# A hybrid decoder layer: the input of chunks 1 to 3 turned by VectorE, the norm's factor applied after the projections

## The chip, the cores and the metric

The kernel runs on one core of a Trainium2 chip. The metric is the device time of one execution in microseconds (us). TensorE (PE, with its weight loads as PEld), VectorE (DVE), ScalarE (ACT), GpSimd (POOL) and SyncE (SP, which issues most of the transfers) each work through a queue of instructions in its written order.

## The reference

One layer on x (1 x 2048 x 1024, float32), cut to what matters:

```python
h = rms_norm(x, attn_norm_g)                  # x * rsqrt(mean(x*x)) * g
z = h @ w_in                                  # q 512, k 128, v 128, gate_b 512, gate_c 512, xc 512
q, k = rms_norm(q, q_norm_g), rms_norm(k, k_norm_g)
y_attn = swa_sink_attention(q, k, v, sinks)   # 8 heads of 64, 2 kv heads, window 128
y_conv = gate_b * short_conv(gate_c * xc, conv_w)      # 3 taps, causal
y = concat(rms_norm(y_attn, attn_out_g), rms_norm(y_conv, conv_out_g))
x = x + y @ w_out
hm = rms_norm(x, mlp_norm_g)
x = x + square(relu(hm @ w_up)) @ w_down      # w_up 1024x4096
```

A matrix product is made in three terms: both operands are split into a high part (rounded to the matmul's type) and a low part (what the rounding left), and `mm3` adds high x high, high x low and low x high in PSUM.

## The kernel before

The sequence is cut into four chunks of CH = 512 tokens, each of NT = 4 tiles of P = 128 rows. Features lie in KD = 8 groups of 128. For each chunk (0 to 3) the "mixers" phase makes the projection, the attention of four blocks, the gated convolution and the out projection. After it come the MLP's up product (line L1401) and down product (L1508), which take the last 70% of the time and which the change does not touch.

The projections need h of a chunk turned, with features on the partitions: two parts (high and low, `h_h`) of 128 x 8 x 512. They have one buffer each, and the convolution of the present chunk reads them to its last matmul (`pb_c`), so h of the next chunk is written after that. `prepare` makes it for chunks 1 to 3. For each of the four row tiles it fetches 128 x 1024 of x in one transfer (`xt_a`, two buffers), has ScalarE take the sum of squares (L273) and GpSimd the reciprocal root, multiplies by the norm's factor and the gain row on VectorE (L280), turns the tile by eight 128x128 transposes on TensorE in two groups of four (`pt_a`, L292, one PSUM bank), copies each group to the high part on ScalarE (L296) and subtracts on VectorE for the low part (L297). Chunk 0 is made apart, at the start: there the transposes are of x itself, the gain is applied in the copy, and the norm's factor (`rs0`) multiplies the projections' outputs; its square lies as a row over the tokens on all partitions (`rs0_row`).

`besides` runs the convolution, `prepare`, the second half of the out projection and the next chunk's projection as a stream of small steps. `mixers` interleaves it with the attention's steps (`fill`). The attention of one block: queries and keys turned (`ptq_b`, `ptk_b`), scores (`psc_b`) copied by ScalarE, masked by VectorE (L646), exponentials by ScalarE (L652), normalised by VectorE (L660), turned (`ptp_b`) and split into `pp_b` (ScalarE L677, VectorE L678) with GpSimd's masks on it (L684), values (`po_b`, L723) and their split. The convolution: gate C (`pc_c`, copied by ScalarE at L773 in chunks 1 to 3, multiplied by `rs0_row` on VectorE in chunk 0), `px_c`, the three taps on VectorE (L790, L792), gate B (`pb_c`), the split `yt_c` (L807, L808), the sum of squares `ssc` (L812, L813).

Weights are read in chunk 0 as raw parts (`raw_wc`, `raw_wx`, `raw_wb`, `raw_wo`), split by ScalarE (L243, L246) and VectorE (L247) into `w_...`, and stored; later chunks read the stored parts (lines L226 to L230). The out projection is `pout`, made in two halves; each result is added to x on VectorE with the branch's norm factor (`rc` for the convolution's, L862).

The order of each engine's queue is set when the kernel is built, by a planner that has its own costs. Steps within `with ahead(i)` have a priority from a table by stage, and the program's order breaks ties. No order is decided while the kernel runs: an engine waits at the instruction that stands next in its queue, and a transfer behind a waiting transfer on SP waits with it.

Of the kernel before, what the change touches and what calls it, by code (L numbers as in the profile page):

```python
# [7 lines left out]
F32 = mybir.dt.float32  # L8
# [4 lines left out]
ALU = mybir.AluOpType  # L13
# [55 lines left out]

CHP = CH + 32  # L70
STEPS = 3
REST = 7
LATER = 250

# [27 lines left out]
def hymba_layer(  # L102
# [44 lines left out]
        [[dram.tile([P, 2, BW], F32, name=f"fop{tb}_{i}_{g}") for g in range(NCG // 2)] for i in range(len(ORDER))]  # L147
        for tb in range(NTB)
    ]
    wds_dram = [[dram.tile([P, 2, BW], F32, name=f"wds{g}_{i}") for i in range(2)] for g in range(NCG // 2)]  # L150

    def bank(tag, name):
# [126 lines left out]
    def scaled(xt, rs, gb):  # L279
        nc.vector.scalar_tensor_tensor(xt, xt, rs, gb, op0=ALU.mult, op1=ALU.mult)  # L280

    def norm(xt, gb, name):

        scaled(xt, norm_stats(xt, name), gb)

    def transposed(xt, dst, t, name, tag="tr"):

        for kk in range(0, KD, 4):
            with ahead(9):
                pt = bank(tag, f"pt_{name}_{kk}")  # L290
                for j in range(4):
                    nc.tensor.transpose(pt[:, j * P : (j + 1) * P], xt[:, (kk + j) * P : (kk + j + 1) * P], ident)  # L292
                p3 = pt.rearrange("p (k t) -> p k t", k=4)
                dh = dst[0][:, kk : kk + 4, t * P : (t + 1) * P]
                dl = dst[1][:, kk : kk + 4, t * P : (t + 1) * P]
                nc.scalar.copy(dh, p3)  # L296
                nc.vector.tensor_tensor(dl, p3, dh.bitcast(F32), op=ALU.subtract)  # L297
            yield

    def raised(xt, dst, name, tag="tr"):  # L300

        for k in range(2):
# [12 lines left out]
    def x_sums(tb, t, b11, b21, b12, b22, t1):  # L315
# [17 lines left out]
    def parts(pool_, tag, name):  # L333
        return [pool_.tile([P, KD, CH], F32R, tag=f"{tag}{s}", name=f"{tag}{s}_{name}", bufs=1) for s in range(2)]

    def prepare(src, r0, gb, dst, name):

        xs = []

        def fetch(t):  # L340
            xt = row("xt", f"xt_{name}_{t}", 2)
            nc.sync.dma_start(xt, src[r0 + t * P : r0 + (t + 1) * P, :])
            with ahead(8):
                norm(xt, gb, f"{name}_{t}")
                xs.append(xt)
# [168 lines left out]
    with tc.tile_pool(name="mix_small", bufs=1) as mix_small, tc.tile_pool(name="mix", bufs=1) as mix:  # L514
# [10 lines left out]
        def project_qkv(c, h, z):  # L525
# [36 lines left out]
            w4 = [w.rearrange("p (k c) -> p k c", k=KD) for w in weights(None, c, "qkv2")]  # L562

            for pc, t in ((0, 0), (0, 1), (1, 0), (0, 2), (0, 3), (1, 1), (1, 2), (1, 3)):
                n = 256 if pc else AW
                ps = bank("mm", f"pz{c}_{pc}_{t}")[:, :n]
                hk = lambda s, k, t=t: h[s][:, k, t * P : (t + 1) * P]
                wk = (lambda s, k: w4[s][:, k, :]) if pc else (lambda s, k: both[k // (KD // 2)][s][:, k % (KD // 2), :])
                for k in range(KD):
                    mm3(ps, lambda s, k=k: hk(s, k), lambda s, k=k: wk(s, k), k == 0, k == KD - 1)  # L570
                    if (k % 2 or not pc) and k < KD - 1:
                        yield
                nc.scalar.copy(z[t][:, pc * AW : pc * AW + n], ps)
                if pc and not t:
                    qk_norm(c * NT, z[0])
                yield
# [169 lines left out]
            nc.vector.tensor_copy(ms, pa[:, :1])  # L746
            rsqrt(dst, ms)

        def conv_pair(c, h, j, yt, ssc):

            nm = f"c{c}_{j}"

# [15 lines left out]
            for i in range(2):  # L768
                ps = bank("mm", f"pc_{nm}_{i}")
                yield from group(hl, ps, i)  # L770
                g = pool.tile([P, CHP], F32, tag="s2", name=f"u_{nm}_{i}", bufs=4)
                if c:
                    nc.scalar.copy(g[:, 2 : CH + 2], ps)  # L773
                else:
                    nc.vector.tensor_tensor(g[:, 2 : CH + 2], ps, rs0_row, op=ALU.mult)
                gc.append(g)
                yield
            hl = weights(cols256(wi, O_X + j * 256), c, f"wx{j}")
# [127 lines left out]
                    x_put(0, t, 2, b[1])  # L906
                yield

        def besides(c, before, h, yt, rc, x1, h_next, z_next):
# [11 lines left out]
            out = out_projection(c, 1, yt, rc, x1)  # L921
            if c + 1 < NCHUNK:
                h_next += parts(pool, "h", f"h{c + 1}")
                steps = prepare(xf, (c + 1) * CH, g_row[0], h_next, f"a{c + 1}")
            else:
                steps = prepare_mlp(gain_row(mlp_norm_g, "g_mlp"))
            for i, _ in enumerate(steps):
                yield
                for j in range(STEPS):
                    next(out, None)  # L930
                    yield
                    if (i, j) == PC:
# [5 lines left out]
                        ms = mix_small.tile([P, NT], F32, tag="msc", name=f"ms_c{c}", bufs=1)  # L938

                        with tc.high_priority(offset=SOON):  # L940
                            if c:
                                nc.vector.tensor_copy(ms, pc[:, :NT])
                                rsqrt(rc, ms)
                            else:
                                nc.vector.tensor_tensor(ms, pc[:, :NT], rs0_2, op=ALU.mult)
                                rsqrt(rc, ms)
                                nc.gpsimd.tensor_tensor(rc, rc, rs0, op=ALU.mult)
            yield from out
            if c + 1 < NCHUNK:
                yield from project_qkv(c + 1, h_next, z_next)  # L950
            else:
                begin_mlp()

        def mixers(c, before, h, z):


            last = c + 1 == NCHUNK
            n_fill = FILL[c]
            stage[0] = c
            at, yt, x1, h_next, z_next = [], [], [], [], []  # L960
            ra = small.tile([P, NT], F32, tag="ra", name=f"ra{c}", bufs=2)
            rc = small.tile([P, NT], F32, tag="rc", name=f"rc{c}", bufs=2)
            steps = besides(c, before, h, yt, rc, x1, h_next, z_next)
            left = out_projection(c, 0, at, ra, x1)

            spare = (NT - 1) * NCT if last else 0
# [43 lines left out]
                        attn_rstd(b, sqa, ra[:, NT - 1 : NT])  # L1010
                    yield

            return rest(), h_next, z_next

        z = []
        for _ in project_qkv(0, h, z):
# [39 lines left out]
        g_row = [gain_row(attn_norm_g, "g_attn")]  # L1056
        left = iter(())
        for c in range(NCHUNK):
            left, h, z = mixers(c, left, h, z)
        for _ in left:  # L1060
            pass

# [485 lines left out]
```

## Time and profile before

| what | us |
| --- | --- |
| median of 3 runs | 1944.46 |
| the runs, lowest to highest | 1941.45 to 1945.74 |
| span of the profiled execution, first to last instruction | 1937.4 |
| median less that span | 7.1 |
| TensorE busy | 1921.2 |
| VectorE busy | 1192.2 |
| ScalarE busy | 836.8 |
| GpSimd busy | 270.1 |

The profiled execution has its span only; what the runs have beyond it is the 7.1 us of the table. In the rows of a profile, "busy" is a sum over a group of instructions and the number behind it the mean of one in ns; what stands last in a row is the engine's idle time just before them, with what ended it. Matmuls overlap one another, so the mean of one is longer than the step from one to the next.

### The profile page before, as it was taken

Reading aid. Unit: us, or ns where it says so; the run is one execution under the profiler, and the core shown is the slowest. Engines: PE = TensorE matmul, PEld = TensorE weight load, DVE = VectorE, ACT = ScalarE, POOL = GpSimd, SP = SyncE. Lnnn points to the kernel's source line nnn. Section 1 sums busy time; section 2 is a strip of 40 time slices with the busy share of each in tenths; the row PEclk is TensorE's granted clock in tenths of the full one; section 3 lists DMA queues with packets and bytes.
Section 4 is the critical chain, followed back from the end, with each engine's and each line's share of the span. In section 5 each row is a group of like instructions: output and inputs, shape, how many; then the busy total and the mean of one; then the engine's idle time right before and its main releaser. Section 6 shows DMA issues by size and latency. Waiting matters only on the chain. (4 is left out here: it accounts for less than half of the span.)

```text
span 1937.4 us, 24882 instructions
## 1 busy us (share of the span) xinstructions
PE 1921.2 (99%) x9089; PEld 1599.6 (83%) x9089; DVE 1192.2 (62%) x1864; ACT 836.8 (43%) x1593; POOL 270.1 (14%) x471
## 2 busy tenths in 40 slices
PE   9999999999999999999999999999999999999999
PEld 9888888887888788888878888888888888888887
DVE  4885657447456769777868766666544334458541
ACT  6564444335344436454555554554422333232320
POOL 2122212312221111222200111101000000100000
PEclk9999999999999999999999999999999999999999
DMA  9774854564473897666665544437964446766631
GB/s 325 276 282 130 329 192 174 201 234 152 186 276 136 271 310 255 215 219 211 212 219 201 179 158 147 162 123 301 370 217 145 149 161 230 264 234 213 206 135 55
DMA packets 211162, 409.63 MB, mean 211 GB/s; under 512 B 18392, under 2 KB 121824, under 8 KB 199264
## 3 DMA queue, kind: packets, MB, share of 16 engines
q1 hardware_dynamic: 182416, 332.52, 49.4%
q0 software_dynamic: 15360, 51.39, 6.9%
q10 hardware_dynamic: 13264, 24.13, 3.3%
q8 instruction: 72, 1.18, 0.2%
q14 instruction: 50, 0.41, 0.1%
HBM read 282.16 MB, written 125.83 MB: 211 GB/s over the span
## 5 line engine op out<-in xcount | busy, mean ns | idle before, releaser
L1401 PE MATMUL u<-op_x,wop 128*128 128x512 f32 x2688 | 617.0, 390 | 1.7 <-DVE wop L387 0.8
L1508 PE MATMUL d<-op_w,op_f 128*128 128x512 f32 x2688 | 609.4, 389 | 0.0
L1401 PEld LDWEIGHTS u<-op_x,wop 128*128 128x128 f32 x2688 | 502.5, 188 | 109.3 <-DVE wop L387 3.0
L1508 PEld LDWEIGHTS d<-op_w,op_f 128*128 128x128 f32 x2688 | 504.5, 188 | 104.8
L370 DVE TENSOR_TENSOR op_f<-op_f 128x1024 fp32r<-128x1024 f32 x112 | 136.9, 1224 | 231.0 <-ACT op_f L369 230.3
L369 ACT CAST op_f<-op_f 128x1024 fp32r<-128x1024 f32 x112 | 117.6, 1052 | 349.2 <-DMA op_f<-fop 348.6
L386 ACT CAST wop<-wu 128x512 fp32r<-128x512 f32 x156 | 96.3, 620 | 102.2 <-PE u L1401 98.2
L387 DVE TENSOR_TENSOR wop<-wu,wop 128x512 fp32r<-128x512 f32 x156 | 107.3, 689 | 38.2 <-DMA wu<-in_w_up_dram 20.1
L1131 POOL DMA_DIRECT2D fop<-s x96 | 52.5, 547 | 435.2 <-DVE s L1134 415.3
L1137 DVE TENSOR_TENSOR u<-u,u 128x512 f32<-128x512 f32 x128 | 87.7, 685 | 22.1 <-PE u L1401 22.1
L370 DVE TENSOR_TENSOR op_w<-raw,op_w 128x1024 fp32r<-128x1024 f32 x56 | 68.4, 1222 | 30.6 <-ACT op_w L369 30.4
L369 ACT CAST op_w<-raw 128x1024 fp32r<-128x1024 f32 x56 | 58.8, 1052 | 48.9 <-PE d L1508 24.5
L652 ACT ACTIVATE sc_b<-sc_b,ngm_b 128x128 f32<-128x128 f32 x128 | 49.6, 390 | 28.7 <-DVE ngm_b L649 28.7
L684 POOL TENSOR_SCALAR_AFFINE_SELECT pp_b<-pp_b 128x512 fp32r<-128x512 f32 x60 | 41.3, 700 | 117.0 <-ACT pp_b L677 63.5
L386 ACT CAST wop<-wu_s 128x512 fp32r<-128x512 f32 x64 | 39.4, 619 | 34.7 <-PE u L1401 32.0
L1350 POOL DMA_DIRECT2D wds<-raw x16 | 8.6, 536 | 324.4 <-DVE raw L1348 324.4
L1143 ACT ACTIVATE u<-u 128x512 f32<-128x512 f32 x64 | 40.4, 632 | 29.8 <-DVE u L1137 26.7
L264 PE MATMUL pout<-w_wo,yt_c 128*128 128x512 f32 x128 | 52.5, 410 | 0.0
L266 PE MATMUL pout<-w_wo,yt_c 128*128 128x512 f32 x128 | 51.9, 406 | 0.0
L265 PE MATMUL pout<-w_wo,yt_c 128*128 128x512 f32 x128 | 51.2, 400 | 0.0
L264 PE MATMUL pout<-w_wo,at_b 128*128 128x512 f32 x128 | 50.2, 394 | 0.2 <-DVE ms_b L746 0.2
L265 PE MATMUL pout<-w_wo,at_b 128*128 128x512 f32 x128 | 50.0, 390 | 0.2 <-DVE w_wo L247 0.2
(256 smaller groups left out, 3123.4 us busy)
## 6 DMA issues: line engine op xcount, KB each, us to landing
op_f<-fop SPq DMA_DIRECT2D x112, 512.0 KB, 4.2
raw<-in_w_down_dram SPq DMA_DIRECT2D x72, 512.0 KB, 4.0
wu<-in_w_up_dram SPq DMA_DIRECT2D x128, 256.0 KB, 3.3
w_wo<-wo SPq DMA_DIRECT2D x24, 1024.0 KB, 6.8
fop<-s POOLq DMA_DIRECT2D x96, 256.0 KB, 2.4
fop<-u ACTq DMA_DIRECT2D x64, 256.0 KB, 2.4
op_x<-xop SPq DMA_DIRECT2D x28, 512.0 KB, 6.8
w_q<-qkv SPq DMA_DIRECT2D x24, 512.0 KB, 6.0
```

The source lines that it names most:

```text
L264: nc.tensor.matmul(ps, st(0), mv(0), start=first, stop=False)
L265: nc.tensor.matmul(ps, st(0), mv(1), start=False, stop=False)
L266: nc.tensor.matmul(ps, st(1), mv(0), start=False, stop=last)
L369: nc.scalar.copy(op[:, 0], raw)
L370: nc.vector.tensor_tensor(op[:, 1], raw, op[:, 0].bitcast(F32), op=ALU.subtract)
L386: splits.append(nc.scalar.copy(hi, blk).ins)
L387: nc.vector.tensor_tensor(lo, blk, hi.bitcast(F32), op=ALU.subtract)
L652: nc.scalar.activation(sc[:, hd, :], sc[:, hd, :], AF.Exp, bias=ngm[:, hd : hd + 1], accum_out=den[:, hd : hd + 1])
L1131: eng.dma_start(fop_dram[tb][ORDER_DOWN.index(i)][n // 2][:, n % 2], b)
L1137: return nc.vector.tensor_tensor(dst, ps, b, op=ALU.add).ins
L1401: nc.tensor.matmul(pt, wops[i][:, a, k, :], xops[tb, p][k // 2][:, b, k % 2, :], start=p not in GOES_ON and k + j == 0, stop=k + j == NB + ...
L1508: nc.tensor.matmul(ps[tb][j], fs[tb][:, a, k, j * P : (j + 1) * P], w[:, b, k, :], start=first and p not in GOES_ON and k + n == 0, stop=l ...
```

## The change

For chunks 1 to 3 `prepare` no longer reads rows of x and turns them on TensorE. It reads x in 16 transfers a chunk (`load_turned`), each filling 32 partitions with 32 rows x 32 floats at a time: 1024 runs of 32 floats. A tile `xt_a` of 128 x 1024 then holds the x of two feature groups (jj and jj+4), such that a transpose of 32x32 blocks on VectorE, 128x512 at a time, makes the feature group turned. The high part is then a ScalarE copy scaled by the gain of the feature (`g_in`), the low part one scaled subtraction on VectorE. The turned x goes through the tile `gb`, in two halves, which held the gain's row before; that row's load goes.

`stats` makes the norm's factors of the next chunk during the convolution of the present one. It reads x once more, in eight pieces of 128x512 through one half of `gb`, squares each in place on ScalarE with the sum kept, and GpSimd makes the factor `rs` and its square, which goes to DRAM and is read back as a row on all partitions (`rs2_row`, in the other half of `gb`).

The factor multiplies the outputs, as in chunk 0: q, k, v in ScalarE's copy, gate C's output by the squared factor on VectorE (ScalarE's copy at L773 goes), and the convolution's norm factor `rc` by `rs`.

```diff
-    def norm(xt, gb, name):
-        scaled(xt, norm_stats(xt, name), gb)
-    def transposed(xt, dst, t, name, tag="tr"):
-        for kk in range(0, KD, 4):
-            with ahead(9):
...
+    def load_turned(xb, src, r0, jj):
+        for pg in range(4):
+            rows = src[r0 : r0 + BW].rearrange("(q i) (k c) -> i k q c", i=TS, k=2)
+            c0 = jj * P + pg * TS
+            nc.sync.dma_start(
+                xb[pg * TS : (pg + 1) * TS].rearrange("p (k q c) -> p k q c", k=2, c=TS), rows[:, :, :, c0 : c0 + TS]
+            )
...
-    def prepare(src, r0, gb, dst, name):
+    def prepare(c, dst, gb):
+        xts = {}
+        def fetch(jj):
+            xts[jj] = row("xt", f"xt_a{c}_{jj}", 2)
+            load_turned(xts[jj], xf, c * CH, jj)
         fetch(0)
         fetch(1)
         yield
+        for jj in range(NB):
+            for k in (jj, jj + NB):
+                xt = xts[jj][:, (k // NB) * BW : (k // NB + 1) * BW]
+                with ahead(9):
+                    dh, dl = (d[:, k] for d in dst)
+                    st = gb[:, k // NB]
+                    nc.vector.transpose(st, xt)
+                    nc.scalar.activation(dh, st, AF.Copy, scale=g_in[k])
+                    nc.vector.scalar_tensor_tensor(dl, st, g_in[k], dh.bitcast(F32), op0=ALU.mult, op1=ALU.subtract)
+                yield
+            if jj + 2 < NB:
+                fetch(jj + 2)
+    def stats(c, rs, gb):
+        xr = gb[:, 1]
+        def fetch(t, i):
+            r = c * CH + t * P
+            nc.sync.dma_start(xr, xf[r : r + P, i * CH : (i + 1) * CH])
+        fetch(0, 0)
+        yield
         for t in range(NT):
-            yield from transposed(xs[t], dst, t, f"{name}_{t}")
-            if t + 2 < NT:
-                fetch(t + 2)
+            ss = small.tile([P, 2], F32, tag="ss2", name=f"ss_a{c}_{t}", bufs=2)
+            for i in range(2):
+                nc.scalar.activation(xr, xr, AF.Square, scale=D**-0.5, accum_out=ss[:, i : i + 1])
+                if t + i < NT:
+                    fetch(t + i, 1 - i)
...
+        nc.gpsimd.tensor_tensor(rs[1], rs[0], rs[0], op=ALU.mult)
+        nc.gpsimd.dma_start(rs2_dram[c].rearrange("(t p) -> p t", p=P), rs[1])
...
-                nc.scalar.copy(z[t][:, pc * AW : pc * AW + n], ps)
+                nc.scalar.activation(z[t][:, pc * AW : pc * AW + n], ps, AF.Copy, scale=rs[:, t : t + 1])
...
-                if c:
-                    nc.scalar.copy(g[:, 2 : CH + 2], ps)
-                else:
-                    nc.vector.tensor_tensor(g[:, 2 : CH + 2], ps, rs0_row, op=ALU.mult)
+                nc.vector.tensor_tensor(g[:, 2 : CH + 2], ps, rs2_row, op=ALU.mult)
...
+            gb = pool.tile([P, 2, CH], F32, tag="gb", name=f"gb{c}", bufs=1)
+            rs2_row = gb[:, 0] if c else rs0_row
+            if c:
+                nc.sync.dma_start(rs2_row, rs2_dram[c].partition_broadcast(P))
...
             for j in range(2):
-                yield from conv_pair(c, h, j, yt, ssc)
+                for i, _ in enumerate(conv_pair(c, h, j, yt, ssc, rs2_row)):
+                    if i % STATS == STATS - 1:
+                        next(sums, None)
+                    yield
```

More of the change, by code (lines that the diff above doesn't have):

```diff
@@ L71 @@
 STEPS = 3
+TS = 32
+STATS = 9
 REST = 7
@@ L149, in hymba_layer @@
     ]
+    rs_dram = [dram.tile([CH], F32, name=f"rs_dram{c}") for c in range(NCHUNK)]
+    rs2_dram = [dram.tile([CH], F32, name=f"rs2_dram{c}") for c in range(NCHUNK)]
     wds_dram = [[dram.tile([P, 2, BW], F32, name=f"wds{g}_{i}") for i in range(2)] for g in range(NCG // 2)]
@@ L907, in prepare_mlp, with besides @@
                 yield
-        def besides(c, before, h, yt, rc, x1, h_next, z_next):
+        def besides(c, before, h, yt, rc, x1, h_next, z_next, rs, rs_next):
             yield from before
             ssc = mix.tile([P, CH], F32, tag="ssc", name=f"ssc{c}", bufs=1)
-            for j in range(2):
-                yield from conv_pair(c, h, j, yt, ssc)
+            gb = pool.tile([P, 2, CH], F32, tag="gb", name=f"gb{c}", bufs=1)
+            rs2_row = gb[:, 0] if c else rs0_row
+            if c:
+                nc.sync.dma_start(rs2_row, rs2_dram[c].partition_broadcast(P))
+            if c + 1 < NCHUNK:
+                rs_next += [small.tile([P, NT], F32, tag=f"rs_a{i}", name=f"rs{i}_a{c + 1}", bufs=2) for i in range(2)]
+            sums = stats(c + 1, rs_next, gb) if c + 1 < NCHUNK else iter(())
+            for j in range(2):
+                for i, _ in enumerate(conv_pair(c, h, j, yt, ssc, rs2_row)):
+                    if i % STATS == STATS - 1:
+                        next(sums, None)
+                    yield
+            for _ in sums:
+                pass
             x1 += [] if c else x0
@@ L923, in besides @@
                 h_next += parts(pool, "h", f"h{c + 1}")
-                steps = prepare(xf, (c + 1) * CH, g_row[0], h_next, f"a{c + 1}")
+                steps = prepare(c + 1, h_next, gb)
             else:
@@ L940, in besides, with mixers @@
                         with tc.high_priority(offset=SOON):
[L941 to L947, printed above, removed]
+                            nc.vector.tensor_tensor(ms, pc[:, :NT], rs[1], op=ALU.mult)
+                            rsqrt(rc, ms)
+                            nc.gpsimd.tensor_tensor(rc, rc, rs[0], op=ALU.mult)
             yield from out
             if c + 1 < NCHUNK:
-                yield from project_qkv(c + 1, h_next, z_next)
+                yield from project_qkv(c + 1, h_next, z_next, rs_next[0])
             else:
                 begin_mlp()
-        def mixers(c, before, h, z):
+        def mixers(c, before, h, z, rs):
             last = c + 1 == NCHUNK
@@ L1011, in rest @@
                     yield
[L1013 removed]
+            return rest(), h_next, z_next, rs_next
         z = []
@@ L1055, in hymba_layer @@
             nc.gpsimd.memset(vd[:, kv, 1, 1 - kv, :].bitcast(F32), 0.0)
-        g_row = [gain_row(attn_norm_g, "g_attn")]
-        left = iter(())
+        left, rs = iter(()), [rs0, rs0_2]
         for c in range(NCHUNK):
-            left, h, z = mixers(c, left, h, z)
+            left, h, z, rs = mixers(c, left, h, z, rs)
         for _ in left:
```

27 lines of the change are left out of this document (7 added, 20 removed).

## The prediction

> **What bounds the kernel now.** I read first the page's head, its busy totals and the chain of waits.
>
> ```profile
> span 1937.4 us, 24882 instructions
> PE 1921.2 (99%) x9089; PEld 1599.6 (83%) x9089; DVE 1192.2 (62%) x1864; ACT 836.8 (43%) x1593; POOL 270.1 (14%) x471
> ...
> PE 46%; DVE 0%; ACT 0%; issue 0%
> ```
>
> TensorE is busy 1921.2 of 1937.4 us and the chain is TensorE's own: 16 us of idle time are all that could be won without taking work from it. The median of the runs, 1944.46 us, is 7.1 us above this span; I add that 7.1 us unchanged to whatever span I work out. Then, by windows, the three stretches in which the changed preparation runs (columns: busy time of PE, weight loads, DVE, ACT, POOL, granted clock, DMA share, GB/s).
>
> ```profile
> 46.00:155.00 109.00, 108.09 (x549) 90.31 (x548) 94.85 (x194) 64.42 (x174) 19.47 (x33) 1.00 0.75 274
> 170.00:326.00 156.00, 154.66 (x790) 129.73 (x789) 100.11 (x203) 72.88 (x197) 36.77 (x61) 1.00 0.60 209
> 340.00:500.00 160.00, 157.57 (x815) 132.49 (x814) 96.45 (x192) 67.03 (x187) 35.91 (x59) 1.00 0.54 201
> ```
>
> TensorE is full in each, at full clock. But VectorE is 87% busy in the first, with DMA at 0.75: there the cover is thin. It is 64% and 60% in the others. So a TensorE microsecond saved counts, and a microsecond that the other engines are late counts too.
>
> **What the change removes.** TensorE's 96 transposes of x go, with what TensorE waited at them (groups of instructions with shapes kept apart; then the waits of PE; then the timeline of PE):
>
> ```profile
> L292 PE MATMUL pt_a<-ident,xt_a 128*128 128x128 f32 x96 | 14.8, 276 | 4.4 <-DVE h_h L297 2.4 <-DVE ms_b L746 1.1 <-DVE xt_a L280 0.9
> ```
> ```profile
> PE pt_a L292 <- DVE h_h L297: 2.4, 4, 1.6
> PE pt_a L292 <- DVE ms_b L746: 1.1, 2, 0.6
> ```
> ```profile
> 147.07 0.39 PE L265 MATMUL pout<-w_wo,yt_c 128*128 128x512 f32 x1
> 147.31 0.60 PE L292 MATMUL pt_a<-ident,xt_a 128*128 128x128 f32 x4
> 147.66 0.48 PE L266 MATMUL pout<-w_wo,yt_c 128*128 128x512 f32 x1
> 147.97 0.40 PE L264 MATMUL pout<-w_wo,yt_c 128*128 128x512 f32 x1
> ```
>
> A matmul step is 0.24 us (147.07 to 147.31). From 147.07 to 147.97 lie two steps and one group of four transposes: 0.90 - 0.48 = 0.42 us a group. 24 groups: 10.1 us, all on the bounding engine. With the 4.4 us of idle time: **14.5 us** is the most that the change can gain.
>
> **What it adds beside TensorE.** Per chunk eight block transposes of 128x512 on VectorE, eight scaled copies on ScalarE (hi), eight scaled subtractions on VectorE (lo); the sums of squares, from a second reading of x in 8 pieces; 12 copies of conv outputs move from ScalarE to VectorE. Rows of the same operations, and of what goes:
>
> ```profile
> L246 ACT ACTIVATE w_wo<-raw_wo,g_y 128x512 fp32r<-128x512 f32 x16 | 10.8, 719 | 0.1
> L247 DVE SCALAR_TENSOR_TENSOR w_wo<-raw_wo,g_y,w_wo 128x512 fp32r<-128x512 f32 x16 | 11.6, 744 | 0.0
> L296 ACT CAST h_h<-pt_a 128x512 fp32r<-128x512 f32 x24 | 14.0, 582 | 21.5 <-PE pt_a L292 21.3
> L297 DVE TENSOR_TENSOR h_h<-pt_a,h_h 128x512 fp32r<-128x512 f32 x24 | 16.5, 688 | 3.8 <-ACT h_h L296 3.3
> L280 DVE SCALAR_TENSOR_TENSOR xt_a<-xt_a,rs_a,g_attn 128x1024 f32<-128x1024 f32 x12 | 16.1, 1341 | 6.1 <-POOL rs_a L189 6.1
> L273 ACT ACTIVATE junk_a<-xt_a 128x1024 bf16<-128x1024 f32 x12 | 12.7, 1060 | 6.5 <-DMA xt_a<-in_x_dram 3.7 <-POOL ms_c L188 2.1 <-DVE y_c L792 0.4
> L773 ACT COPY u_c<-pc_c 128x512 f32<-128x512 f32 x12 | 7.0, 586 | 12.7 <-PE pc_c L266 12.5
> L790 DVE TENSOR_SCALAR y_c<-u_c,cw 128x512 f32<-128x512 f32 x14 | 6.8, 486 | 1.4 <-POOL halo L788 0.5
> L660 DVE TENSOR_TENSOR sc_b<-sc_b,den_b 128x1024 f32<-128x1024 f32 x14 | 17.1, 1222 | 0.3
> L812 ACT ACTIVATE y_c<-y_c 128x512 f32<-128x512 f32 x11 | 6.9, 631 | 9.5 <-DVE yt_c L808 8.7 <-POOL ms_b L188 0.8
> ```
>
> No row shows the block transpose. Its bounds are 0.49 (the one-input 128x512, L790) and 1.22 us (the 128x1024, L660); I take 0.69, nearest to the two-input 128x512 of L297. VectorE, over three chunks: 24 x (0.69 + 0.74) + 12 x 0.69 - 24 x 0.69 - 12 x 1.34 = +10 us; ScalarE: 24 x 0.72 + 24 x (0.63 + 0.19 for reading the accumulator, the L652 row below) - 24 x 0.58 - 12 x (1.06 + 0.19) - 12 x 0.59 = +1 us. Spread over 425 us that is nothing, and the squares and the gate's product cost nothing while this slack covers them; without cover their price would be these 10 us of VectorE. The Trainium skill, in "VectorE: DVE Perf Modes", The three transpose paths, gives 311 ns for 128x128 bf16 on VectorE; an estimate from it, 4 x 311 ns, is 1.24 us, by which the 14 transposes that stand on the path below would bring 8 us more; no row here can show which is right.
>
> The loads: each of 16 a chunk moves 128 KB in 1024 runs of 32 floats, 64 packets on each of 16 DMA engines.
>
> ```profile
> q1 hardware_dynamic: 182416, 332.52, 49.4%
> ...
> q10 hardware_dynamic: 13264, 24.13, 3.3%
> ```
> ```profile
> wu<-in_w_up_dram SPq DMA_DIRECT2D x128, 256.0 KB, 3.3
> ```
>
> From q1 a packet of 1823 bytes costs 0.494 x 1937.4 x 16 / 182416 = 84 ns, the upper bound for a run of 128 B; the share that goes with bytes alone, 128/1823 of it, 6 ns, is the lower. The wu loads (512 runs of 512 B, landed 3.3 us after issue) fit the low part, so I take some 20 ns: 64 x 20 = 1.3 us a load, 20 us a chunk. In the first stretch that makes DMA 0.75 x 109 + 20 = 102 of 109 us: no reserve, but no bound yet.
>
> **What it moves: the order.** This is the term that decides. The planner fixes each engine's queue when the kernel is built; compared instruction by instruction, the changed queue of SP has the 16 small loads, waiting for VectorE's transposes, ahead of weight loads, and the engines behind it are written accordingly. Hi and lo of the next chunk can be written only after the last conv matmul, since their tile is single. Before, ScalarE had the first w_wo split behind one chain of attention copies only and no hi work; after, its queue from the conv's end of chunk 0 reads:
>
> ```
> hi hi, yt_c, o_b x2, qt, kw x2, vz, vd, at, square of y_c, vz, first piece of w_wo (first matmul of the out projection)
> ...
> pp x2, vz, o_b, vd, hi x2, exp x3, second w_wo (second half of the out projection)
> ```
>
> Rows for these, and for VectorE's queue:
>
> ```profile
> L652 ACT ACTIVATE sc_b<-sc_b,ngm_b 128x128 f32<-128x128 f32 x112 | 43.5, 390 | 21.3 <-DVE ngm_b L649 21.3
> L652 ACT ACTIVATION_READ_ACCUMULATOR sc_b<-sc_b,ngm_b 128x1 f32 x112 | 21.0, 188 | 0.0
> L684 POOL TENSOR_SCALAR_AFFINE_SELECT pp_b<-pp_b 128x512 fp32r<-128x512 f32 x60 | 41.3, 700 | 117.0 <-ACT pp_b L677 63.5 <-PE po_b L723 42.5 <-DVE pp_b L678 10.2
> L807 ACT CAST yt_c<-y_c 128x512 fp32r<-128x512 f32 x14 | 8.7, 620 | 20.6 <-DVE y_c L804 20.5
> L698 ACT CAST vz<-z 128x128 fp32r<-128x128 f32 x28 | 8.3, 298 | 33.5 <-PE po_b L723 33.2
> L862 DVE SCALAR_TENSOR_TENSOR x<-pout,rc,x 128x512 f32<-128x512 f32 x32 | 23.8, 745 | 3.3 <-PE pout L266 3.1
> L646 DVE COPY_PREDICATED sc_b<-later,psc_b 128x128 f32<-128x128 int32 x112 | 26.3, 297 | 17.9 <-ACT sc_b L643 17.8
> L746 DVE COPY ms_b<-pa_b 128x1 f32<-128x1 f32 x16 | 2.4, 151 | 17.8 <-PE pa_b L744 17.8
> L699 DVE TENSOR_TENSOR vz<-z,vz 128x64 fp32r<-128x64 f32 x28 | 9.5, 339 | 26.6 <-ACT vz L698 26.5
> ```
>
> Chunk 0. First line: 2 x 0.72 + 0.62 + 3 x 0.58 + 5 x 0.30 + 0.62 + 0.63 + 0.72 = 7.3 us of ScalarE, against some 2 us of attention matmuls that TensorE has meanwhile: it waits 5.3, and 1 more for the lo half (0.74, then the hand-over). Second line: 0.30 + 0.58 + 0.30 + 1.44 + 3 x 0.58 + 0.72 = 5.1, and 1 for lo: 6. The probabilities of blocks 2 and 3 stand with hardly a matmul between copying and use: cast 0.58, subtraction 0.69, two selects of 0.70 make 2.7 and 2.7. The last w_wb split stands behind score copies: 2. Sum 19.7.
>
> Chunk 1. Here the whole attention of block 3 is written ahead of the second half of the out projection, because SP has that half's weights behind loads that wait for VectorE's transposes. VectorE has, from the last conv gate to the last subtraction of probabilities: 21 pieces of 128x512 at 0.69, six of them transposes (14.5); 12 scaled ones at 0.745, eight of them lo (8.9); 8 predicated copies at 0.30 (2.4); 2 of 1024 columns at 1.22 (2.4); 16 narrow pieces, taken at 0.30 (4.8); 8 tiny ones at 0.16 (1.3): 34.3 us. Then two selects 1.4, five matmuls 1.2, and 45 matmuls of the out projection 10.8 before the next projection: 47.7 us. TensorE's own work in that stretch is 138 matmuls and transposes, some 33 us. It waits 14.7.
>
> Chunk 2. The same half stands ahead of block 3's probabilities; I find only one bare chain of probabilities and a late hi: 4.
>
> Sum: 19.7 + 14.7 + 4 - 14.5 = **+24 us**: 1968 us.
>
> **Rivals.**
> *The queues catch up* (faster). Written order costs only where the work ahead isn't done earlier. If ScalarE and VectorE run through the hi and lo work while TensorE still has matmuls, each stall shrinks; it decides when the stalls fall below 14.5 us in all. Without them 1944.5 - 14.5 = 1930; with half of them, 1949. For it: ScalarE's 59% in the first stretch. Against: hi cannot begin before the conv's end, and the queues are in order. Chance 0.11, and 0.05 for a draw.
> *Runs of 128 B as dear as a packet of 1823 B* (slower still). 64 x 84 ns = 5.4 us a load, 86 us a chunk. DMA time in the stretches becomes 0.75 x 109 + 86 = 168, 94 + 86 = 180 and 86 + 86 = 172 us: 59 + 24 + 12 = 95 us over, less 14.5: 2025 us. It decides from about 27 us of room, 26 ns a packet, in the first stretch. Against: wu's 3.3 us. Chance 0.10. The Trainium skill, "DMA: Bandwidth & Descriptors", Specifications, puts the least transfer for line rate at 512 B, with read-modify-write below; no row of before has runs of 128 B, so the new loads' landing will show it.
> *The change does nothing to the path*: the 96 transposes are gone from the written queue, so this is left only as the draw above.
>
> **How the numbers follow.** Forecast of stalls over 14.5 us: 0.74, its own range 1949 (half the stalls) to 1990 (half as much again, with the transpose's upper bound). Catching up 0.11, a draw 0.05, dear runs 0.10. The range to 2005 takes in the dear runs up to some 62 ns a packet (64 us a chunk, 37 over the room of the first stretch, on top of the forecast); down to 1941 it takes in the draw. About 0.2%, 3.9 us, is what a measurement of this kernel can tell from no change. Faster 0.11, same 0.05, slower 0.84.
>
> **What would show it.** Right: no L292 group; PE's waits in chunks 0 and 1 at pout on the w_wo splits and at values on the selects, 15 to 20 us in each; VectorE's transposes near 0.7 us. Wrong: PE's idle time in the three stretches under 15 us; or the waits all on the new x loads (then it is the dear runs); or a projection output late because the row of squared factors lands late.

## The result, and the profile after

The changed kernel takes 1997.78 us (median of four runs, 1994.42 to 2004.33) against 1944.24 us for the kernel before in the same session: a ratio of 1.0285, with a 95% interval of 1.0266 to 1.0305. It is 53.5 us slower. The forecast was slower by 24 us. The direction was right, and so were the two largest places; two costs, together as large as the forecast's own error, are nowhere in its sum. The profiled execution is the fastest of the four (1994.42 us); the other three have mean clocks of 0.987 to 0.991. The page's head, totals and chain, and the clock line of both kernels (after, then before):

```profile
span 1992.7 us, 24829 instructions
PE 1946.6 (98%) x8993; PEld 1602.5 (80%) x8993; DVE 1202.3 (60%) x1888; ACT 838.1 (42%) x1605; POOL 276.3 (14%) x480
...
PE 87%; DVE 5%; DMA 3%; ACT 2%; POOL 2%; SPq 1%; issue 1%; ACTq 0%; DVEq 0%; POOLq 0%
```
```profile
core 0: 1992.7 us, clock 0.993
```
```profile
core 0: 1937.4 us, clock 1.000
```

Three things are to be seen. TensorE's idle time rose from 16.2 to 46.1 us, which was forecast in kind. Its busy time rose too, by 25.4 us, although it has 96 instructions fewer: on average an instruction takes longer. And the mean granted clock is no longer 1.000.

Where in time the 55.3 us between the two profiled spans arise is read from the starts of the first projection matmul of each chunk and from the first and last start of the up and the down product (before, then after; "A to B" is the first and last start):

```profile
L264 PE MATMUL pz<-w_q,h_h x64: 387/389/480, 154.6 to 353.7; 128*128 128x512 f32 x64
L264 PE MATMUL pz<-w_q,h_h x32: 387/389/480, 326.0 to 353.7; 128*128 128x512 f32 x32
L264 PE MATMUL pz<-w_q,h_h x32: 389/389/484, 498.8 to 525.8; 128*128 128x512 f32 x32
L1401 PE MATMUL u<-op_x,wop x2688: 387/389/506, 691.7 to 1323.6; 128*128 128x512 f32 x192
L1508 PE MATMUL d<-op_w,op_f x2688: 388/389/389, 1323.9 to 1932.9; 128*128 128x512 f32 x192
```
```profile
L268 PE MATMUL pz<-w_q,h_h x64: 387/389/776, 174.0 to 390.7; 128*128 128x512 f32 x64
L268 PE MATMUL pz<-w_q,h_h x32: 387/389/776, 361.3 to 390.7; 128*128 128x512 f32 x32
L268 PE MATMUL pz<-w_q,h_h x32: 389/389/484, 532.6 to 559.0; 128*128 128x512 f32 x32
L1428 PE MATMUL u<-op_x,wop x2688: 387/392/502, 729.9 to 1375.0; 128*128 128x512 f32 x192
L1535 PE MATMUL d<-op_w,op_f x2688: 387/389/404, 1375.3 to 1988.4; 128*128 128x512 f32 x192
```

Chunk 0 loses 174.0 - 154.6 = 19.4 us, chunk 1 another 15.9, chunk 2 gains 1.5, the rest of the mixers loses 4.4. Then the up product, whose code is untouched, takes 13.2 us longer (start to the start of the down product) and the down product 4.1. In the up product the median matmul takes 392 ns instead of 389.

The waits of PE in the first two places, from 110 to 174 us and from 300 to 361.3 us:

```profile
PE pout L268 <- ACT w_wo L250: 8.0, 2, 4.1
PE po_b L746 <- POOL pp_b L707: 1.2, 2, 0.6
```
```profile
PE po_b L746 <- DVE pp_b L701: 5.0, 2, 3.3
PE po_b L746 <- ACT pp_b L700: 1.1, 2, 0.8
```

They stand where the forecast put them, at the out projection's weight split on ScalarE in chunk 0 and at the probabilities on VectorE in chunk 1, but they are shorter: from 110 to 174 us TensorE is idle for 11.1 us where 19.7 were forecast, and from 300 to 361.3 us for 7.9 where 14.7 were. Ahead of the first wait, ScalarE runs the queue that the prediction wrote out, from the two hi copies to the split (its first two rows and the split; the matmul starts at 135.67 us):

```profile
127.99 1.34 ACT L349 ACTIVATE h_h<-gb,g_in 128x512 fp32r<-128x512 f32 x2 [0.67 <-PE pb_c L270]
129.24 0.60 ACT L827 CAST yt_c<-y_c 128x512 fp32r<-128x512 f32 x1
...
134.89 0.72 ACT L250 ACTIVATE w_wo<-raw_wo,g_y 128x512 fp32r<-128x512 f32 x1
```

But behind such a wait the matmuls run slowly. Windows of 10 us of the changed kernel (the seventh column is the granted clock):

```profile
130.00:140.00 10.00, 5.33 (x19) 4.41 (x19) 7.49 (x15) 8.71 (x20) 1.85 (x3) 0.66 0.00 0
140.00:150.00 10.00, 9.78 (x37) 7.91 (x38) 8.84 (x18) 1.92 (x4) 2.09 (x4) 0.83 0.90 263
```

From 140 to 150 us TensorE is busy nearly all the time and 37 instructions fall into the window; from 170 to 180 us, at a clock of 1.00, there are 47. The timeline shows the step from one matmul to the next, at 141 and at 147 us:

```profile
141.34 0.63 PE L268 MATMUL pout<-w_wo,yt_c 128*128 128x512 f32 x1
141.76 0.63 PE L269 MATMUL pout<-w_wo,yt_c 128*128 128x512 f32 x1
...
147.15 0.39 PE L270 MATMUL pout<-w_wo,yt_c 128*128 128x512 f32 x1
147.38 0.39 PE L268 MATMUL pout<-w_wo,yt_c 128*128 128x512 f32 x1
```

That is 0.42 us against 0.23. In windows of 1 us the clock reads 0.50 from 134 to 143 us. Five more such stretches, of some 3.4 us each, follow the waits that end at 161, 208, 348, 382 and 706 us; elsewhere up to the MLP the clock is 1.00. A mean clock of 0.993 over 1992.7 us is a loss of 0.007 x 1992.7 = 13.9 us; some 1.3 us of it fall into the waits themselves, where nothing runs.

The new operations themselves:

```profile
L348 DVE STREAM_TRANSPOSE gb<-xt_a 128x512 f32<-128x512 f32 x24 | 16.1, 693 | 0.5 <-DMA xt_a<-in_x_dram 0.5
L349 ACT ACTIVATE h_h<-gb,g_in 128x512 fp32r<-128x512 f32 x24 | 16.5, 719 | 16.7 <-DVE gb L348 9.4 <-PE pb_c L270 7.3
L350 DVE SCALAR_TENSOR_TENSOR h_h<-gb,g_in,h_h 128x512 fp32r<-128x512 f32 x24 | 18.0, 774 | 0.2
```
```profile
q1 hardware_dynamic: 234352, 339.08, 50.5%
...
xt_a<-in_x_dram SPq DMA_DIRECT2D x48, 128.0 KB, 4.9
```

The block transpose takes 693 ns and waited 0.5 us in all for its loads; TensorE never waited for one.

### The profile page after: what moved, and what is told of

The parts are those of the page before. It is cut to its first block, busy times and chain, and to the rows that moved or that the text cites. A ratio compares the mean times of both kernels' runs of the same rounds, so it can differ in the third digit from the quotient of the medians.

```text
span 1992.7 us, 24829 instructions
## 1 busy us (share of the span) xinstructions
PE 1946.6 (98%) x8993; PEld 1602.5 (80%) x8993; DVE 1202.3 (60%) x1888; ACT 838.1 (42%) x1605; POOL 276.3 (14%) x480
## 4 chain that ended last, share of the span: by engine, by line
PE 87%; DVE 5%; DMA 3%; ACT 2%; POOL 2%; SPq 1%; issue 1%; ACTq 0%; DVEq 0%; POOLq 0%
PE d L1535 31%; PE u L1428 30%; PE pout L268 2%; PE pout L269 2%; PE pout L270 2%; PE pc_c L269 1%; PE pc_c L270 1%; PE pc_c L268 1%; PE pz L268 1%; PE pz L269 1%; PE pz L270 1%; PE pb_c L268 1%; PE pb_c L269 1%; PE pb_c L270 1%; PE px_c L268 1%; PE px_c L270 1%
## 5 line engine op out<-in xcount | busy, mean ns | idle before, releaser
L1428 PE MATMUL u<-op_x,wop 128*128 128x512 f32 x2688 | 628.0, 394 | 5.0 <-ACT wop L409 4.4
L1535 PE MATMUL d<-op_w,op_f 128*128 128x512 f32 x2688 | 613.5, 390 | 0.0
L675 ACT ACTIVATE sc_b<-sc_b,ngm_b 128x128 f32<-128x128 f32 x128 | 49.7, 393 | 29.9 <-DVE ngm_b L672 29.9
```

Of the source, the lines that this page charges most:

```text
L675: nc.scalar.activation(sc[:, hd, :], sc[:, hd, :], AF.Exp, bias=ngm[:, hd : hd + 1], accum_out=den[:, hd : hd + 1])
L1428: nc.tensor.matmul(pt, wops[i][:, a, k, :], xops[tb, p][k // 2][:, b, k % 2, :], start=p not in GOES_ON and k + j == 0, stop=k + j == NB + ...
L1535: nc.tensor.matmul(ps[tb][j], fs[tb][:, a, k, j * P : (j + 1) * P], w[:, b, k, :], start=first and p not in GOES_ON and k + n == 0, stop=l ...
```

## The experiments

All times are medians; each run had the kernel before beside it on the same chip (1942.5 to 1943.4 us). The changed kernel had it at 1944.24 us, so a gain counted from 1997.78 us is too large by up to 1.8 us.

**Addresses: e1, e2, e8, e9.** The up product is unchanged code at full clock, yet slower. What the change alters there is where tiles lie: its new small tiles (`rs_a`, `ss2`) push every large tile up by 128 bytes a partition, except the MLP operand tiles that are laid out from the far end of the memory. In the built programs the near tiles start at 0 modulo 512 bytes before and at 128 after; the far ones at 0 in both. e1 pads the changed kernel back, with no other difference:

```diff
     warm = const.tile([P, 1], F32, name="warm")
+    const.tile([P, 96], F32, name="pad")
```

> The changed kernel with one unused tile of 384 bytes a partition more, so that every large tile starts at the address it has in the kernel before modulo 512 (the change's new small tiles had moved them all by 128 bytes); order of all queues unchanged. Address theory: the matmul step in the MLP (0.2302 us in the up product after, 0.2251 before; 0.2281 and 0.2267 in the down product) goes back, up product 10 us and down product 4 us shorter, some more in the mixers: 14 to 20 us off, about 1981 us. Theory that the whole loss comes from the order of the queues, or from the small runs of the loads: no change, 1998 us, and the up product's step stays 0.230 us.

Measured: 1976.63 us, 21 off. The mixers take as long as without the pad (the up product starts at 730.6 us, in the changed kernel at 729.9); the up product is 16.4 us shorter and the down product 4.1. e2 does the reverse in the kernel before, with a pad of 32 floats:

> The kernel before with one unused tile of 128 bytes a partition more; order of all queues unchanged. Address theory: the up and the down product get the steps of the changed kernel, 14 to 20 us more, about 1960 us. Other theories: 1944 us.

Measured: 1959.44 us, 17 more than before (ratio 1.0090, 1.0073 to 1.0107), with no change in any queue's order. The same window of the up product (before, after, e1, e2):

```profile
1150.00:1200.00 50.00, 50.00 (x223) 41.39 (x222) 35.32 (x55) 26.29 (x44) 5.96 (x11) 1.00 0.45 150
```
```profile
1150.00:1200.00 50.00, 50.00 (x218) 40.50 (x217) 33.63 (x52) 24.84 (x41) 4.88 (x9) 1.00 0.47 151
```
```profile
1150.00:1200.00 50.00, 50.00 (x223) 41.39 (x222) 34.61 (x54) 26.09 (x44) 6.35 (x12) 1.00 0.48 162
```
```profile
1150.00:1200.00 50.00, 50.00 (x218) 40.55 (x217) 32.43 (x50) 25.16 (x42) 6.51 (x12) 1.00 0.51 163
```

223 instructions of TensorE in 50 us against 218, at a clock of 1.00 in all four: the second column's count follows the pad and nothing else. (The count takes in those that reach over the window's ends.) e8 pads the kernel before by 64 floats (256 bytes), e9 by 32 floats at the near end and 96 at the far end, so that both groups of tiles stand at 128.

```diff
     fill = ops.tile([P, 120], F32, tag="fill", name="fill")
+    ops.tile([P, 96], F32, name="pad_ops")
```

> The kernel before with an unused tile of 256 bytes a partition (e2 had 128), order unchanged. Address theory in the form that two operands of one matmul must agree modulo 512 bytes: as e2, 1959 us. In the form that they must agree modulo 256: 1943 us, the step of the up product 0.227 us.

> The kernel before with the 128 bytes of e2, and 384 bytes more at the far end, so that the operand tiles of the MLP that are laid out from that end move by 128 bytes modulo 512 too; order unchanged. Address theory in its relative form (the two operands of a matmul must agree): both now stand at 128, step of the up product 0.227 us, 1943 us. In its absolute form (each must stand at a multiple of 256): as e2 or worse, 1959 to 1970 us.

Measured: e8 1943.16 us, e9 1940.90 us (ratio 0.9986, 0.9977 to 0.9995). So 128 bytes are dear between the two groups, 256 are not, and 128 in both are not: what counts is how the operands of a matmul stand to each other, not where each stands. The changed kernel's own trace says the same within one run. Some operand tiles of the MLP lie among the near ones, so of the seven products that make up the up product the first two in `ORDER` have both operands near, and the other five have one near and one far. Between the starts of single matmuls the median is 227 ns in those two and 232 to 233 ns in the five; in the kernel before it is 227 in all seven. In the down product it is 227 where the two tiles start alike and 232 where they do not. Some 2400 steps that are 6 ns longer make 14 us. One run limits the rule: in e7 below the near tiles start at 448 modulo 512, and there all seven products take 229 to 231 ns, also the two with both operands near. So it is shown for distances of 0, 128 and 256 bytes only. Why is left open; no run looked into it.

**Order: e3, e4.** e3 keeps the 16 loads and their bytes but reads whole rows, which makes the planner write another order; e4 keeps the 32-float runs and issues them from ScalarE's queue.

```diff
-            rows = src[r0 : r0 + BW].rearrange("(q i) (k c) -> i k q c", i=TS, k=2)
...
+            r = r0 + jj * P + pg * TS
+            nc.sync.dma_start(xb[pg * TS : (pg + 1) * TS], src[r : r + TS])
```
```diff
-            nc.sync.dma_start(
+            nc.scalar.dma_start(
                 xb[pg * TS : (pg + 1) * TS].rearrange("p (k q c) -> p k q c", k=2, c=TS), rows[:, :, :, c0 : c0 + TS]
```

> The changed kernel with the 16 loads a chunk kept in number and bytes, but each reading whole rows of x of 4 KB instead of runs of 32 floats (so h is made from x in another arrangement). The planner then writes another order: the loads no longer stand ahead of weight loads on SP. Order theory (my prediction's): idle time of TensorE falls from 46 to 20 to 28 us, and the stretches with a granted clock under 1.00 go with it; 25 to 35 us off, about 1965 us, with the matmul step of the up product still 0.230 us. Theory that the transfers in small runs take the time: about the same gain, so this run tells of order and runs together, and the next one tells them apart.

> The changed kernel with the 16 loads a chunk, in runs of 32 floats as they are, issued from ScalarE's queue instead of SP's, so that weight loads on SP do not stand behind them. Order theory: about half to two thirds of the idle time that the change added goes (idle 46 to 30 us), with part of the clock's loss: 15 to 25 us off, about 1978 us. Theory of small runs: no gain, 1998 us, or a loss, as ScalarE now issues 48 transfers.

Measured: e3 1970.36 us, 27 less than the changed kernel; e4 1981.77 us, 16 less, both at the changed kernel's addresses. TensorE's idle time falls from 46.1 to 29.7 us in e3 and 33.5 in e4, a little less than expected, and the clock does not come back: 0.994 and 0.989 in the profiled runs, against 0.993. The 8.0 us at the splits of `w_wo` are gone in both (0.8 us is the most that is left there); the longest waits left in the mixers (e3, then e4):

```profile
PE pc L964 <- DVE ssc L830: 3.5, 3, 1.8
PE po_b L743 <- ACT pp_b L697: 3.4, 1, 3.4
```
```profile
PE po_b L746 <- ACT pp_b L700: 4.1, 1, 4.1
```

The transfers' price can be read from e3's page:

```profile
q1 hardware_dynamic: 186736, 339.08, 51.6%
```

The same bytes, 47,616 packets fewer, and the share of the span is 0.516 x 1968.2 = 1016 us against 0.505 x 1992.7 = 1006: the small runs took no more of the DMA engines' time than rows of 4 KB, and they landed no later (4.9 us after issue in the median, 5.5 in e3). The Trainium skill ("DMA: Bandwidth & Descriptors", Specifications) puts the least transfer for line rate at 512 B; here, where the queue's packets take half of the DMA engines' time, runs of 128 B show no loss against rows of 4 KB. e11 adds e1's pad to e3:

> e3 (the loads as whole rows, the planner's other order) at e1's addresses. If address and order add up: 1970 less 17 to 21, 1949 to 1953 us, with 10 to 15 us more idle time than the kernel before. If e3's remainder was something else: 1960 us or more.

Measured: 1951.88 us. Address and order add up (1970.4 - 18.5); 8 to 9 us over the kernel before are left, and they were not taken apart further.

**One part alone: e6, e7.** e6 keeps the statistics, the row of squared factors and the scaled outputs, and turns x on TensorE from whole rows (at e1's addresses); the gain on the input is left out. Its `prepare` has the loop of the kernel before:

```diff
+                    for j in range(4):
+                        nc.tensor.transpose(pt[:, j * P : (j + 1) * P], xts[t][:, (kk + j) * P : (kk + j + 1) * P], ident)
...
-                    nc.vector.transpose(st, xt)
```

> One part of the change alone, at e1's addresses: the second reading of x for the sums, the squared factor's row and the factor on the projections' outputs stay, but x of chunks 1 to 3 comes in rows of 4 KB (four transfers a chunk) and is turned by TensorE in groups of four, as before; the gain on the input is left out. Order theory with the loads as the cause: no small loads on SP, so the waits go back to those of the kernel before: idle time under 20 us, about 1945 us. Theory that the statistics, their row through DRAM and the gate's product on VectorE cost: 1955 us or more.

Measured: 1948.41 us, ratio 1.0023 (1.0013 to 1.0032). Applying the factor to the outputs and reading x twice cost some 5 us together in this order; the other 28 us of e1's loss come with the turned loads and the work on them, as the planner places them. e7 leaves the second reading and its sums out of e1 and uses chunk 0's factors:

```diff
-            sums = stats(c + 1, rs_next, gb) if c + 1 < NCHUNK else iter(())
+            sums = iter(())
+            rs_next[:] = [rs0, rs0_2]
```

> The padded changed kernel (e1) without the second reading of x and its sums (chunk 0's factors are used for all chunks). Theory that the loads in 32-float runs, as the planner prices them, set the order: most of the loss stays, 1960 to 1972 us. Theory that the 24 further transfers and squares are the cause: about 1935 to 1945 us.

Measured: 1993.15 us, more than e1 and outside both expectations. The run says little: the planner's new order has ScalarE stand before a weight load in chunk 0, a wait that no other run has, and without the small tiles the large ones start at 448 modulo 512, so the address cost is partly back (first to last start of the up product 638.0 us, 628.7 in e1). The wait of PE, and ScalarE's timeline:

```profile
PE pz L269 <- ACT z L567: 8.7, 1, 8.7
```
```profile
52.49 0.62 ACT L248 CAST w_wc<-raw_wc 128x512 fp32r<-128x512 f32 x1 [15.74 <-DMA qkv<-w_qkv]
53.01 0.47 ACT L567 ACTIVATE z<-pz,rs 128x256 f32<-128x256 f32 x1
```

**Clock: e5.** e1 with 20 needless matmuls in the place of its longest wait.

```diff
+                    for _ in range(20 if half and not dh and not c and not t and not i else 0):
+                        nc.tensor.matmul(ps, ys[NCT - 1][:, 0, :P], ys[NCT - 1][:, 0, :], start=True, stop=True)
                     mm3(ps, y, lambda s, i=i: w4[s][:, i, :], i == 0, i == NCT - 1)
```

> The padded changed kernel (e1) with 20 needless matmuls of 512 columns (4.5 us) put on TensorE between the end of chunk 0's convolution and the first matmul of the out projection, in the place of its longest wait (4.1 us); they write a bank that the real product then overwrites, and the rest of TensorE's queue keeps its order. Clock theory: the wait costs more than its length, since the stretch behind it ran with a granted clock of 0.66 (130 to 140 us in the changed kernel); with TensorE kept busy the clock stays at 1.00 there and the run is some 4 to 5 us shorter than e1, about 1972 us, although 4.5 us of work were added. Theory that the clock fell for another reason: 1977 us, the clock in that stretch as in e1. Theory that the wait is all there is and the matmuls come on top: 1977 to 1981 us.

Measured: 1972.84 us (1969.01 to 1974.70) against e1's 1976.63 (1974.62 to 1978.49): work was added and the median fell by 3.8 us, though the two ranges just touch, with four runs each. Windows of e1's profiled run, then of e5's:

```profile
130.00:140.00 10.00, 4.76 (x18) 3.34 (x16) 7.97 (x14) 8.75 (x19) 2.14 (x2) 0.79 0.00 0
140.00:150.00 10.00, 9.77 (x36) 8.11 (x36) 8.32 (x17) 3.52 (x8) 2.91 (x5) 0.70 0.71 212
```
```profile
130.00:140.00 10.00, 8.21 (x40) 6.68 (x41) 8.31 (x16) 8.71 (x21) 2.94 (x5) 1.00 0.00 0
140.00:150.00 10.00, 10.00 (x38) 8.01 (x38) 8.72 (x18) 2.19 (x5) 1.60 (x3) 0.83 0.93 271
```

The clock stays at 1.00 through the filled wait; a shorter dip follows at a later, smaller one. So the local effect is shown. For the whole kernel it rests on the medians: the two profiled runs have the same span (1972.9 and 1973.0 us) and the same mean clock of 0.992, since e5 lost at later waits what it had kept here. The other three runs of e5 have clocks of 0.993 to 0.996, those of e1 0.988 to 0.991. The Trainium skill ("TensorE: Matmul & The Clock Gate", What's actually happening) describes a gate with a half-rate state that follows an idle window of some 3.4 us. The windows agree with a drop to half rate behind idleness; but a wait of 2.4 us already showed one, and one of 3.35 us in the up product, ending at 773 us, showed none (clock 1.00 from 768 to 778 us). The length of a wait alone did not decide it. In the changed kernel, the wait of 2.4 us and the window behind it:

```profile
PE ptq_b L631 <- DVE z L620: 2.4, 1, 2.4
```
```profile
210.00:220.00 10.00, 10.00 (x65) 9.43 (x65) 6.32 (x12) 8.11 (x17) 2.96 (x4) 0.91 0.43 149
```

**Can the change be made to pay: e10, e12.** e10 is e1 with the planner's inputs set again: the priorities of chunks 0 to 2, some filling steps, and the queues of the loads.

```diff
-    (40, 0, 160, -10, 10, 0, 80, 10, -20, 30, 0, 300),
-    (220, 0, -60, -50, 40, 0, 270, -20, 50, 280, 0, 0),
-    (200, 0, 10, -50, 40, 0, 260, -20, 70, 280, 0, 10),
+    (160, 0, 100, -10, 10, 0, 140, 10, -10, 10, 0, 180),
+    (230, 30, -60, -50, 40, 0, 210, -30, 80, 30, 10, 200),
+    (200, -120, 10, -50, 40, 0, 260, -20, -100, 60, 0, 10),
...
-            nc.sync.dma_start(
+            (nc.sync, nc.scalar, nc.gpsimd)[(2, 0, 1, 1)[jj]].dma_start(
```

> The padded changed kernel (e1) with every part of the change kept, loads in 32-float runs too, and only the planner's inputs changed: priorities and numbers of filling steps in chunks 0 to 2, and the loads issued from GpSimd's queue (first of four), SP's (second) and ScalarE's (the others), chosen such that no weight load stands behind them and no split of out-projection weights behind the hi and lo work. Order theory: the waits go, the clock stays up, and the 10.1 us of transposes become visible: 1932 to 1940 us, faster than before. Theory that the small runs, VectorE's added work or the second reading cost by themselves: 1955 us or more, with waits on the new operations.

Measured: 1944.99 us, ratio 1.0007 (0.9998 to 1.0016): every part of the change is in, small runs too, and it is level with the kernel before. The order theory's rival falls; the forecast gain did not come. Its page, its longest wait of PE, and ScalarE's timeline at that place:

```profile
PE 1916.6 (99%) x8993; PEld 1596.0 (82%) x8993; DVE 1199.0 (62%) x1888; ACT 836.9 (43%) x1605; POOL 280.6 (14%) x492
```
```profile
PE ptq_b L621 <- ACT sc_b L656: 5.3, 1, 5.3
```
```profile
75.13 0.63 ACT L358 ACTIVATE gb<-gb 128x512 f32<-128x512 f32 x1 [3.47 <-DMA gb<-in_x_dram]
75.66 0.19 ACT L358 ACTIVATION_READ_ACCUMULATOR gb<-gb 128x1 f32 x1
75.88 0.92 ACT L656 COPY sc_b<-psc_b 128x256 f32<-128x256 f32 x3
```

TensorE's busy time is now below that of before, but a square of the second reading waits for its piece with the score copies behind it. A third of the clock's loss (3.4 of 10.3 us) lies behind that wait, and half (5.1 us) at the kernel's start, from 8 to 19 us, at waits of 2.1 and 4.2 us for a weight split and for chunk 0's x. e12 reads the sums from whole rows through two buffers, with priorities and filling steps set once more:

```diff
-        xr = gb[:, 1]
+            xts[t] = row("xt", f"xt_s{c}_{t}", 2)
+            nc.sync.dma_start(xts[t], xf[c * CH + t * P : c * CH + (t + 1) * P, :])
...
-                nc.scalar.activation(xr, xr, AF.Square, scale=D**-0.5, accum_out=ss[:, i : i + 1])
+            nc.scalar.activation(xts[t], xts[t], AF.Square, scale=D**-0.5, accum_out=ss[:, :1])
```

> e10 with the sums of squares taken from whole rows: four transfers of 512 KB and four squares of 1024 columns a chunk, through the two buffers that the small loads use later, instead of eight pieces through one buffer; priorities set again for it. e10's one long wait in the mixers was 5.3 us at 71 us, where ScalarE stood at a square that waited for its piece, with score copies behind it. Theory that the single buffer makes that wait: it goes, with the drop of the clock behind it, 6 to 8 us off: 1936 to 1939 us, 0.2 to 0.4 per cent faster than before. Theory that chunk 0's transfers as a whole are too many (share 0.75 before): another wait of 4 us or more on a transfer in 40 to 110 us, 1943 to 1948 us.

Measured: 1943.87 us, ratio 1.0007 (0.9997 to 1.0016). The wait behind the square is gone, and others stand in its place. The time is that of the second theory, its sign is not: none of the long waits is on a transfer (PE's waits, from the start to 800 us):

```profile
PE pa_b L756 <- DVE o_b L751: 5.0, 1, 5.0
PE ptq_b L620 <- DVE z L609: 3.0, 1, 3.0
```
```profile
core 0: 1945.4 us, clock 0.994
```

The clock's 0.006 alone is 11.7 us in this run of 1947.12 us, about as much as the transposes were worth; the eleven runs have clocks of 0.994 to 0.997, the kernel before beside them 0.997 to 1.000. No version beat the kernel before.

## Why the prediction was wrong, by its own steps

The step that failed is the sum: it held stalls and transposes and nothing else, and 24 us came out where 53.5 were measured. It put two terms at nothing without a reason, the clock behind a wait (some 13 us) and the place of the MLP's operands in memory (17 to 21 us). In order:

- **Transposes removed, 10.1 us, and their waits.** Kept. The group is gone; e10, with the clock's loss in it (0.005 x 1943.3 = 9.7 us), still has 4.6 us less busy time than before.
- **Prices of the new operations.** The block transpose was taken at 0.69 us and measured 693 ns; hi 0.72, measured 719; lo 0.74, measured 774. The Trainium skill's figure ("VectorE: DVE Perf Modes", The three transpose paths) had given an estimate of 1.24 us; the measurement decides against that estimate.
- **The loads.** Taken at some 20 ns a packet. Between before and after, q1's share went from 957 to 1006 us of 16 engines with 51,936 packets more: 49.1 x 16 / 51,936 = 15 ns, the second reading of x included. The rival of dear runs was rightly kept small.
- **Stalls from the written order, 38.4 us.** The named places were right in chunks 0 and 1, the sizes too large. Idle time rose by 29.9 us, of which 3.3 lie in the up product (5.0 us of waits against 1.7); with the 4.4 us of waits that went, 31.0 us of new waits in the mixers stand against 38.4. In chunk 0 the two `w_wo` waits were 4.1 and 3.9 us where 6.3 and 6 were forecast, and those at the probabilities 1.7 where 5.4 were. In chunk 2 the place was wrong: 4 us were expected at the probabilities and a late hi, and what came was 3.0 us where the queries are turned and 2.2 at the out projection; chunk 1 has 2.4 us of the first kind too, which the forecast lacks. e4 and e10 show the cause: the same operations in another order lose the waits at the splits, though others come in their place.
- **The clock: missing from the sum.** Every wait was priced at its length. The mean clock of 0.993 adds 13.9 us, and e5 shows for one wait that filling it keeps the clock up. The rows of before had 1.00 throughout, and the forecast took that for a constant; in the changed kernel the clock fell behind six of the waits, and three of these it had itself forecast. How much clock goes with how much idle time stays open: e4 has less idle time than the changed kernel and a lower clock.
- **The addresses: missing from the sum.** The MLP was taken as untouched since no line of it changes. e1 gives 21 us, e2 17; in the two product groups 617.0 to 628.0 and 609.4 to 613.5 us of busy time are 15 of it, in the matmuls whose operands start 128 bytes apart.

Idle time 29.9, transposes -10.1, clock 13.9 and the products' steps 15.1 make 48.8 of the 55.3 us between the two spans; 6.5 us stay unassigned, some 8 if the clock's loss inside the waits is not counted twice. They lie in the mixers, and they are not the addresses, since e1's pad left the mixers' time as it was.

Of the signs that were to show the forecast right, the 15 to 20 us at the named waits in each of chunks 0 and 1 did not come (9.7 and 6.1 us). None of those that were to show it wrong appeared: TensorE's idle time from 46 to 532.6 us was 30.3 us, not under 15, and none of its waits fell on the new loads or on the row of squared factors. Two more costs went without a sign. The one that would have caught both is TensorE's busy time against its instruction count. That 1997.78 us lies within the stated range is luck: above 1990 us the room was kept for dear loads, and the loads were not dear.

## What to carry to other kernels

Where TensorE is 99% busy, price a new wait above its length, and look whether the clock holds behind it. After any edit that adds a tile, however small, compare the start addresses of the operands of the long matmul phases as well as the code: 128 bytes cost here more than the edit could gain. And where a planner writes the order, the form of a transfer can move everything behind it: e3 changed only the loads, and the waits at the weight splits went.

## What the runs showed of the hardware that was not expected

A matmul of 512 columns whose two operand tiles start 128 bytes apart (modulo 512) takes a step of 232 to 233 ns in the median of the changed kernel's up product, against 227 ns at equal starts in the same run and in the kernel before; at 256 bytes apart there is no loss (227 ns in e8). Six waits of 2.0 to 4.1 us on TensorE were followed by stretches with a granted clock of 0.50, one of 10 us and five of 3.4; waits of 2.0 us (ending at 411 us) and 3.35 us (at 773 us) were not. Between the kernel before and the changed one, each packet more, runs of 128 bytes for the most part, came to 15 ns of a DMA engine's time.
